# Reloads, sums and result tiles moved in the value projections of a streaming encoder layer

## The chip, the cores and the metric

The kernel runs on one core of one Trainium2 chip. The metric is device time in microseconds, the median of the runs shown. A core has five engines that run their own queues side by side: TensorE (PE, matmuls and transposes, with its weight loads shown apart as PEld), VectorE (DVE), ScalarE (ACT), GpSimd (POOL) and SyncE (SP), which issues most DMAs. An engine works through its queue in order and waits on semaphores for the others.

## The reference

One layer of an encoder over 1024 prompt frames and 64 sample frames (1088 columns in all), model width 1024:

```python
h = rms_norm(x, norm_w) @ w_in                      # 1024 -> 6144 columns
sb_q, sb_k, sb_v, sb_z, cb_q, cb_k, cb_v, cb_z, g_sb, g_cb = split(h)
cb_q, cb_k = rms_norm(cb_q, q_norm_w), rms_norm(cb_k, k_norm_w)   # per head of 64
o_sb = stick_breaking(sb_q, sb_k, sb_v)             # the sample also sees 512 cached keys
o_cb = band_attention(cb_q, cb_k, cb_v, rel_bias)   # chunks of 64, eight chunks to the left
b_sb = (o_sb * silu(sb_z)) @ w_proj_sb
b_cb = (o_cb * silu(cb_z)) @ w_proj_cb
y = x + (sigmoid(g_sb) * b_sb + sigmoid(g_cb) * b_cb) @ w_out
```

It returns y and the new keys and values of both branches, for the prompt and for the sample. All is float32.

## The kernel before, in words

Every float32 product is made of three matmuls on a high and a low part: x = xh + xl and w = wh + wl, and xh*wh + xl*wh + xh*wl is summed in PSUM. A high part is a copy by ACT into a rounded type; the low part is source minus high, by DVE or POOL. The kernel also saves products by Strassen-like sums: a 2x2 block product becomes seven products of sums of blocks, so weights and activations are added before, and results combined after, on DVE.

The order of the work on every engine is the order in which the code is written (a manual schedule). The projections run in three stages.

* **Natural stage** (loop `for i in range(2, nb)`, to about 151 us). For each 256-column block i and each of nine row tiles (index `ti`, with `TO` giving the row tile t, the sample first) PE does 24 matmuls (16 for the sample) into `acc`. `evac_nat` takes squares (ACT, L386), the product with the norm weights and the row sums (DVE, L387 and L389) and the inverse root (POOL, L305 and L306). One tile later `norm_nat` scales the rows (ACT, L398, four pieces), and three tiles later `post_nat` transposes them on PE (L421) into a PSUM tile (`pt`, `pk` or `b2`) and splits the result (ACT L425, DVE L426). Between these, weight quarters for the next stage are loaded (`load_quad`, L523), summed (`sum_w`, L453) and split: `split_quad` makes the high part at once on ACT (L531) and leaves the low part in a list, `lows`, which `put_lows` empties at its next call (L183), on the engine given.
* **Value stage** (`ORDER`, about 151 to 220 us). Twelve steps q, each a product of one weight sum with one activation sum: 48 matmuls at L865, in four parts (q, 0) to (q, 3), and `part(at)` issues the other engines' work ahead of each part. The last four `post_nat` calls fall in the parts of step 0. Activation sums `t2` and `t3` are built late, slice by slice: `fetch(e, ...)` reloads a partial sum from DRAM (`d_t1`, L223), `late_add` adds two activations on DVE (L229 and L230, or L232 and L233), and `late_put` splits it (ACT L238, DVE L183). Results are combined on DVE: L747 into `made`, `u`; L750 into a tile `o` (two buffers in pool `nu`) that SP stores (L719, L721, L723). `sample` makes the sample's rows (L732), and `fold` adds their two halves into an `o` tile (ACT L348, DVE L349).
* **Transposed stage** (from about 220 us). Blocks of 128 columns, seven products each, matmuls at L997. `load_raw` (L466) loads the weights, `presum` (L478) adds them, `prep` splits them (ACT L512, POOL L513). The first five blocks are prepared from parts of the value stage on.

Tiles live in pools that close and give their place to later ones. Where it matters here: at (1, 0) the PSUM pools of `acc`, `pt` and `pk` close and `psB`, with the banks `b1` and `b3` of the value stage, takes their place; at (1, 1) the pool of `hl` closes and the quarters `r00` and `r10` (pool `rw`) are loaded over it, so SP issues their loads only after the stores out of `hl` have landed. At (11, 0) `ndx` with the tiles `dl` closes and `ws` takes its place. `wraw` has two buffers, `d` and `dl` two each.

After the projections come both attentions (about 525 to 820 us) and the output projections; the change does not touch them.

## Time and profile before

| | us |
|---|---|
| median of 3 runs | 961.02 (960.94, 961.02, 962.56) |
| the profiled execution | 961.81 |
| its span, first to last instruction | 960.0 |
| PE busy in the span | 946.9 |
| DVE, ACT, POOL busy | 597.1, 498.7, 383.5 |

How to read a page: the span is cut into busy time per engine; groups of instructions carry their line, engine, operation and tiles (written<-read), and idle time ahead of them stands with what ended it. In a list of waits the row "PE b L865 <- DVE wlo L183: 2.5, 1, 2.5" says that a matmul of line 865 waited 2.5 us in total, once, at most 2.5, for DVE's low part. In a row by time, the start and the duration come first, and "[2.52 <-DVE wlo L183]" is the idle time before it with what ended it. Rows of windows give the stretch, its length, then busy time of PE, PEld, DVE, ACT and POOL with the number of instructions, then the granted clock (1.00 is full), the share of the 16 DMA engines that were busy, and GB/s. "SPq" rows are DMA issues in SP's queue.

### The profile page before, as it was taken

Reading aid. Unit: us, or ns where it says so; the run is one execution under the profiler, and the core shown is the slowest. Engines: PE = TensorE matmul, PEld = TensorE weight load, DVE = VectorE, ACT = ScalarE, POOL = GpSimd, SP = SyncE. Lnnn points to the kernel's source line nnn. Section 1 sums busy time; section 2 is a strip of 40 time slices with the busy share of each in tenths; the row PEclk is TensorE's granted clock in tenths of the full one; section 3 lists DMA queues with packets and bytes.
Section 4 is the critical chain, followed back from the end, with each engine's and each line's share of the span. In section 5 each row is a group of like instructions: output and inputs, shape, how many; then the busy total and the mean of one; then the engine's idle time right before and its main releaser. Section 6 shows DMA issues by size and latency. Waiting matters only on the chain.

```text
span 960.0 us, 20496 instructions
## 1 busy us (share of the span) xinstructions
PE 946.9 (99%) x7547; PEld 900.2 (94%) x7547; DVE 597.1 (62%) x1173; ACT 498.7 (52%) x1151; POOL 383.5 (40%) x386
## 2 busy tenths in 40 slices
PE   9999999899999999999999999999999999999998
PEld 8999999899999999999999987888988988999998
DVE  6656777856454564543332388777777875498735
ACT  7667775323443433333432376667886874565220
POOL 3276665005444566655541200111331112677541
PEclk9999999999999999999999999999999999999999
DMA  7737775574656555556523997679799933852642
GB/s 258 250 129 274 270 250 189 178 230 135 184 165 200 177 164 178 172 158 180 160 91 106 276 251 200 187 184 249 219 302 259 242 102 102 265 172 78 216 136 76
DMA packets 177705, 182.78 MB, mean 190 GB/s; under 512 B 30713, under 2 KB 160125, under 8 KB 177478
## 3 DMA queue, kind: packets, MB, share of 16 engines
q1 hardware_dynamic: 166182, 166.60, 58.1%
q10 hardware_dynamic: 8608, 8.20, 2.6%
q0 software_dynamic: 2816, 6.69, 2.2%
q8 instruction: 60, 0.98, 0.4%
q14 instruction: 39, 0.32, 0.1%
HBM read 117.79 MB, written 63.64 MB: 189 GB/s over the span
## 4 chain that ended last, share of the span: by engine, by line
PE 79%; DMA 6%; DVE 5%; ACT 3%; POOL 2%; issue 1%; SPq 1%; ACTq 1%; DVEq 0%; POOLq 0%
PE b L997 30%; PE o L1519 7%; PE z L1422 7%; PE acc L573 7%; PE pt L1475 7%; PE b L1844 6%; PE acc L1273 5%; PE b L1315 5%; PE acc L1166 2%; PE b L573 1%; DMA d_csbT<-hc 1%; PE b L865 1%; DMA sq<-d_qsbT 1%; POOL rsn L306 1%; DMA ks<-d_ksbT 1%
## 5 line engine op out<-in xcount | busy, mean ns | idle before, releaser
L1475 PE MATMUL pt<-ident,be 128*128 128x128 f32 (+1 forms) x568 | 87.1, 277 | 0.9 <-ACT wT L1484 0.6
L1444 DVE TENSOR_TENSOR_SCAN be<-be,imp 128x128 f32<-128x128 f32 (+7 forms) x64 | 82.7, 1339 | 8.4 <-ACT be L1425 8.3
L1422 PE MATMUL z<-ks,sq 128*128 128x320 f32 (+5 forms) x384 | 87.7, 338 | 0.0
L1484 ACT ACTIVATE wT<-pt 128x512 f32<-128x512 f32 (+3 forms) x123 | 57.1, 497 | 43.8 <-PE pt L1475 43.7
L1475 PEld LDWEIGHTS pt<-ident,be 128*128 128x128 f32 (+1 forms) x568 | 66.2, 140 | 13.8 <-issue 5.3
L997 PE MATMUL b<-xm,wlox 128*128 128x256 f32 (+1 forms) x336 | 76.0, 286 | 0.0
L1005 DVE TENSOR_TENSOR u<-b,s 128x256 f32<-128x256 f32 (+1 forms) x56 | 24.1, 439 | 70.6 <-PE b L997 68.2
L1422 PEld LDWEIGHTS z<-ks,sq 128*128 128x128 f32 x384 | 63.5, 190 | 2.2 <-ACT be L1425 0.9
L1519 PE MATMUL o<-wT,vp 128*64 128x256 f32 (+1 forms) x608 | 64.2, 356 | 0.0
L1519 PEld LDWEIGHTS o<-wT,vp 128*64 128x64 f32 x608 | 40.3, 136 | 22.4 <-issue 5.4
L513 POOL TENSOR_TENSOR wlox<-wraw,wlox 128x512 fp32r<-128x512 f32 x19 | 27.4, 1440 | 76.3 <-ACT wlox L512 76.3
L997 PEld LDWEIGHTS b<-xm,wlox 128*128 128x128 f32 x336 | 56.8, 188 | 0.0
L1447 ACT ACTIVATE be<-be,sm 128x640 f32<-128x640 f32 (+5 forms) x68 | 47.2, 694 | 18.0 <-DVE sm L1446 17.9
L1070 POOL DMA_DIRECT2D d_osb<-zt x20 | 10.9, 543 | 100.9 <-DVE zt L1533 44.4
L513 POOL TENSOR_TENSOR whix<-ws,whix 128x512 fp32r<-128x512 f32 x28 | 37.0, 1320 | 34.6 <-ACT whix L512 30.7
L513 POOL TENSOR_TENSOR wlo<-ws,wlo 128x512 fp32r<-128x512 f32 x28 | 38.9, 1389 | 27.4 <-ACT wlo L512 25.1
L1425 ACT ACTIVATE be<-z 128x384 f32<-128x384 f32 (+6 forms) x104 | 48.1, 517 | 3.4 <-PE z L1422 2.9
L1435 ACT ACTIVATE be<-be,sm 128x640 f32<-128x640 f32 (+5 forms) x68 | 47.3, 696 | 3.8 <-DVE sm L1427 3.3
L1315 PE MATMUL b<-og,whi 128*128 128x384 f32 (+1 forms) x192 | 46.7, 327 | 0.0
L899 ACT ACTIVATE hl<-u 128x256 f32<-128x256 f32 (+1 forms) x40 | 17.0, 432 | 55.8 <-issue 16.7
L997 PE MATMUL b<-t0h,whix 128*128 128x256 f32 (+1 forms) x224 | 44.7, 289 | 0.6 <-POOL whix L513 0.6
L398 ACT ACTIVATE qn<-qn,rsn 128x64 f32<-128x64 f32 (+1 forms) x144 | 38.2, 339 | 13.7 <-POOL rsn L306 13.2
(447 smaller groups left out, 3315.6 us busy)
## 6 DMA issues: line engine op xcount, KB each, us to landing
wraw<-in_w_in_dram SPq DMA_DIRECT2D x34, 512.0 KB, 4.7
wrawx<-in_w_in_dram SPq DMA_DIRECT2D x16, 512.0 KB, 4.4
sq<-d_qsbT SPq DMA_DIRECT2D x32, 192.0 KB, 4.9
sq<-d_qcbT SPq DMA_DIRECT2D x32, 192.0 KB, 5.0
xt<-in_x_prompt_dram SPq DMA_DIRECT2D x8, 512.0 KB, 5.1
d_kcbT<-hl SPq DMA_DIRECT2D x8, 512.0 KB
d_qcbT<-hl SPq DMA_DIRECT2D x8, 512.0 KB
d_ksbT<-hl SPq DMA_DIRECT2D x16, 256.0 KB, 2.7
```

The costliest lines, as they stand in the source:

```text
L513: G.tensor_tensor(out=t[:, 1], in0=src, in1=t[:, 0].bitcast(F32), op=OP.subtract)
L573: TE.matmul(ps, x, w, start=first, stop=last, skip_group_check=i < 2)
L997: TE.matmul(ps[:, :m], w[:, hl_, k], right[s](x)[:, k, a:b], start=s < 3 and k == 0 and e == 0, stop=k == 3 and e == 2, skip_group_check=s ...
L1273: TE.matmul(ps[:, :e - a], w[:, p, cw], g[:, a:e], start=m % 12 == 0, stop=m % 12 == 11)
L1315: TE.matmul(pp[uu][:, :n], w[:, p, uu * 128:uu * 128 + 128], g[:, a:e], start=p == 0 and m == 0, stop=p == NPAIR - 1 and m == 2)
L1422: TE.matmul(z[:, :m], s[:, e, q0:q0 + 128], ks[:, h, o + x:o + y], start=(e, h) == parts[0], stop=(e, h) == parts[-1])
L1425: A.activation(be[:r, x:y], z[:r, :m], AF.Sigmoid, scale=-0.125)
L1444: V.tensor_tensor_scan(be[:r, n - 1::-1], be[:r, n - 1::-1], im[:, ::-1], 0.0, op0=OP.mult, op1=OP.max)
L1475: TE.transpose(pt[:kr, x, :r], be[:r, kb * 128:kb * 128 + kr], ident[:r, :r])
L1484: A.activation(w[:, sl:sl + m, q0:q0 + r], pt[:, :m, :r], AF.Copy)
L1519: TE.matmul(o[hd * 64:hd * 64 + 64, c0:c1], vv[:kr, kb, hd * 64:hd * 64 + 64], wT[b, p, j, hd, s // 4][:kr, s % 4, c0:c1] if j < 4 else wT ...
L1844: TE.matmul(ps[:, t], left[s](xs_, k)[:, ts_], wt_[:, k], start=s < 3 and t == k == e == 0, stop=k == 3 and e == 2, skip_group_check=s > 2 ...
```

## The change

In the natural stage's last block: the sums of weight quarters are made one or two tiles earlier, the low part of the first is made by DVE and no longer by POOL, the split of quarter 3 stands ahead of the last tile's `evac_nat` with its low part on DVE, and row tile 6 transposes into `pk`, not `pt`. In the value stage: `fetch(2)` stands ahead of the quarters and goes to the `d` tiles of pool `tq`, `fetch(3)` goes there too, later, `fetch(4)` and `fetch(5)` go to `dl`, the last two to `d`; the reload of quarter (0, 1, 1) moves from (7, 0) to (2, 1); `load_raw(2)` moves from (9, 2) to (11, 1). The two results of step 9 go to `dl` tiles, the first result of step 11 and the fold of the second sample to `made` tiles allocated anew at (10, 1). The low part of block 1 is made by DVE. The core of the diff:

```diff
-            if raw1[:2] == (nb - 1, 7):
+            if raw1[:2] == (nb - 1, 7) and t != 6:
                 pt = psT.tile([128, 4, 128], F32, name="pt")
...
+                if (i, ti) == (nb - 1, 8):
+                    split_quad(3, quad[0, 0, 1])
+                    put_lows()
                 got = evac_nat(i, t, ps)
...
-                if (i, ti) == (nb - 1, 2):
+                if (i, ti) == (nb - 1, 1):
                     for n in (1, 2):
                         made[n] = pn.tile([128, 4, 256], F32, name=f"made{n}", bufs=1)
                     sum_w(made[1], quad[0, 0, 1], quad[0, 1, 1], OP.add)
                     load_quad(0, 1, 0, wpool, "wraw", 2)
+                if (i, ti) == (nb - 1, 2):
+                    sum_w(made[2], made[1], quad[0, 0, 0], OP.subtract)
+                    split_quad(0, made[2])
                 if (i, ti) == (nb - 1, 4):
-                    sum_w(made[2], made[1], quad[0, 0, 0], OP.subtract)
-                    split_quad(0, made[2], G)
-                if (i, ti) == (nb - 1, 5):
                     sum_w(quad[0, 0, 0], quad[0, 0, 0], quad[0, 0, 1], OP.subtract)
                     split_quad(1, made[1])
+                if (i, ti) == (nb - 1, 6):
+                    sum_w(quad[0, 1, 0], quad[0, 1, 0], made[2], OP.subtract)
                 if (i, ti) == (nb - 1, 7):
-                    sum_w(quad[0, 1, 0], quad[0, 1, 0], made[2], OP.subtract)
                     load_quad(1, 1, 1, pn, "made1", 1)
...
-                if (i, ti) == (nb - 1, 8):
-                    split_quad(3, quad[0, 0, 1], G)
-                    put_lows()
...
-                put_s(j, 1, fold(nu.tile([128, 512], F32, name="o")[0:64], ps))
+                lo = made[1][0:64, 0:2].rearrange("p t n -> p (t n)") if j else nu.tile([128, 512], F32, name="o")[0:64]
+                put_s(j, 1, fold(lo, ps))
...
-            v = nu.tile([128, 512], F32, name="o")
+            if (j, s) == (1, 4):
+                v = nd.tile([128, HF], F32, name="dl")[:, :512]
+            elif (j, s, c) == (0, 5, 0):
+                v = made[2][:, 0:2].rearrange("p t n -> p (t n)")
+            else:
+                v = nu.tile([128, 512], F32, name="o")[:]
...
             elif at == (1, 1):
+                fetch(2, tq, "d")
                 p1hx.close()
...
                 load_quad(1, 0, 0, rw, "r00", 1)
-                fetch(2, nd, "dl")
                 load_quad(1, 1, 0, rw, "r10", 1)
-                fetch(3, nd, "dl")
...
                 split_quad(4, made[1])
+                fetch(3, tq, "d")
                 late_add(2)
...
                 for e in (4, 5):
-                    fetch(e, tq, "d")
+                    fetch(e, nd, "dl")
+                load_quad(0, 1, 1, wpool, "wraw", 2)
...
                 for e in (6, 7):
-                    fetch(e, nd, "dl")
+                    fetch(e, tq, "d")
...
                 split_quad(10, quad[1, 1, 1])
-                load_quad(0, 1, 1, wpool, "wraw", 2)
...
                 load_raw(1)
-                load_raw(2)
+            elif at == (10, 1):
+                for n in (1, 2):
+                    made[n] = pn.tile([128, 4, 256], F32, name=f"made{n}", bufs=1)
...
                 presum(1)
-                prep(1)
+                prep(1, V)
+            elif at == (11, 1):
+                load_raw(2)
```

What it moves, at three places. First DVE, from the split of row tile 3 (`hl<-pk`, the end of the natural stage) to that of row tile 7; the new low part is that of quarter 3, and L387 with L389 are the norm steps of tile 7:

```order
 L426 TENSOR_TENSOR hl<-pk,hl 128x2x128
+L183 TENSOR_TENSOR wlo<-wraw,whi 128x1024
 L387 TENSOR_TENSOR qn<-acc,wqk 128x256
 L389 TENSOR_REDUCE msn<-sqn 128x4
 L426 TENSOR_TENSOR hl<-pt,hl 128x2x128 x2
-L747 TENSOR_TENSOR made_296<-b_2571,made_296 128x512
-L426 TENSOR_TENSOR hl<-pt,hl 128x2x128
+L749 TENSOR_TENSOR made_296<-b_2571,made_296 128x512
+L426 TENSOR_TENSOR hl<-pk,hl 128x2x128
 L183 TENSOR_TENSOR wlox<-wraw,whix 128x1024
 L426 TENSOR_TENSOR hl<-pt,hl 128x2x128
```

The low part of quarter 3 has come ahead of tile 7's norm, and tile 6's transposes are read from `pk`.

Second SP's queue at parts (1, 1) to (2, 1), before. The first two rows are the last stores out of `hl`; `r` are the quarters, `d` and `dl` the reloads, `u` the partial result:

```order
L53 DMA d_qcbT_68<-hl 256x1x512
L53 DMA d_qcbT_69<-hl 256x1x512
L523 DMA r_2702<-in_w_in_dram 128x4x256
L223 DMA dl<-d_t_129 128x544
L523 DMA r_2706<-in_w_in_dram 128x4x256
L223 DMA dl<-d_t_130 128x544
L787 DMA u_2710<-d_s_126 128x1024
L223 DMA d<-d_t_127 128x544
```

And the same place in the change:

```order
L53 DMA d_qcbT_68<-hl 256x1x512
L53 DMA d_qcbT_69<-hl 256x1x512
L223 DMA d<-d_t_129 128x544
L523 DMA r_2704<-in_w_in_dram 128x4x256
L523 DMA r_2706<-in_w_in_dram 128x4x256
L793 DMA u_2708<-d_s_126 128x1024
L223 DMA d<-d_t_130 128x544
L223 DMA dl<-d_t_127 128x544
L223 DMA dl<-d_t_128 128x544
L523 DMA wraw<-in_w_in_dram 128x4x256
```

The first reload has passed both quarters, the second has fallen behind them and behind `u`, and the late quarter `wraw` has come up.

Third DVE at the results of steps 7, 9 and 10 (`b` are PSUM banks), in the change; before, the rows with `dl` and `made_3196` wrote `o`:

```order
L757 TENSOR_TENSOR o<-b_3049,made_2513 128x512
L757 TENSOR_TENSOR o<-b_3080,made_2513 128x512
L757 TENSOR_TENSOR dl<-b_3120,u_2709 128x512
L183 TENSOR_TENSOR wlox<-wraw,whix 128x1024
L757 TENSOR_TENSOR dl<-b_3155,u_2709 128x512
L757 TENSOR_TENSOR o<-b_3120,u_2708 128x512
L757 TENSOR_TENSOR o<-b_3155,u_2708 128x512
L349 TENSOR_TENSOR made_3196<-acc,made_3196 64x256
L478 TENSOR_TENSOR ws<-wraw 128x512
```

The order is the old one; the tiles written are others.

## The prediction

> **What bounds the kernel now.** I read the page's busy line first, then the waits of TensorE, then busy time by windows, then the order of time around each wait.

> ```profile
> PE 946.9 (99%) x7547; PEld 900.2 (94%) x7547; DVE 597.1 (62%) x1173; ACT 498.7 (52%) x1151; POOL 383.5 (40%) x386
> ...
> PE b L865 <- DVE wlo L183: 2.5, 1, 2.5
> PE pt L421 <- DVE hl L426: 1.9, 1, 1.9
> PE b L997 <- POOL whix L513: 0.6, 1, 0.6
> PE b L865 <- issue: 0.6, 1, 0.6
> PE b L865 <- DVE o L750: 0.3, 1, 0.3
> ...
> 168.00:180.00 12.00, 9.48 (x69) 9.29 (x69) 9.01 (x12) 3.43 (x4) 0.00 (x0) 0.86 0.64 232
> 180.00:200.00 20.00, 20.00 (x172) 20.00 (x172) 19.76 (x26) 7.38 (x9) 0.00 (x0) 1.00 0.37 122
> ```

> PE (TensorE) is busy for 946.9 of 960.0 us: it is the bound, and a change that leaves its matmuls as they are can win only its idle time and its slow time. The change edits only the stretch from about 135 to 230 us, and there the five waits above are all of PE's idle time. The first window row has a granted clock of 0.86: slow time too. The second says what to fear: in 180 to 200 VectorE (DVE) is busy 19.76 of 20 us, so once PE stops waiting DVE has little to give.

> **The wait at 155 (sums sooner, own bank for one transpose).** Rows by time:

> ```profile
> 152.00 1.07 ACT L398 ACTIVATE qn<-qn,rsn 128x64 f32<-128x64 f32 x4 [2.60 <-POOL rsn L306]
> 155.11 1.04 ACT L531 ACTIVATE whi<-wraw 128x1024 fp32r<-128x1024 f32 x1
> 156.58 1.06 ACT L398 ACTIVATE qn<-qn,rsn 128x64 f32<-128x64 f32 x4
> 157.80 1.05 ACT L531 ACTIVATE whix<-wraw 128x1024 fp32r<-128x1024 f32 x1
> 158.89 1.23 DVE L183 TENSOR_TENSOR wlox<-wraw,whix 128x1024 fp32r<-128x1024 f32 x1 [0.52 <-ACT whix L531]
> 160.03 0.42 DVE L426 TENSOR_TENSOR hl<-pt,hl 128x256 fp32r<-128x256 f32 x1
> 147.34 2.40 POOL L183 TENSOR_TENSOR wlo<-made,whi 128x1024 fp32r<-128x1024 f32 x1
> 154.89 1.01 POOL L306 TENSOR_TENSOR rsn<-rsn,half 128x4 f32<-128x4 f32 x1
> 156.92 0.44 PE L421 MATMUL pt<-ident,qn 128*128 128x128 f32 x2 [1.90 <-DVE hl L426]
> 161.13 0.28 PE L865 MATMUL b<-whix,t0h 128*128 128x256 f32 x1
> ```

> PE waits at 156.92 because tile 6's transposes need a `pt` bank that tile 4 still holds. The change gives tile 6 the `pk` bank, which tile 3 leaves earlier: that wait goes. What is late next is tile 7, whose transposes come twelve matmuls on (12 x 0.115 us), at about 156.5. Its normalised rows come from ACT (L398, 156.58 to 157.64 before). Two things now pull at that row. POOL's 2.40 us lo part (147.34) goes to DVE, at 1.22 us; the rsqrts of tiles 5 and 6 no longer queue behind it, so ACT's 2.60 us of idle at 152.00 shrinks. Against that, the 1.04 us split (155.11) moves ahead of tile 7's Square on ACT, and its lo part (1.22) ahead of tile 7's product and reduce on DVE. Adding the rows: PE ends tile 7's matmuls at the old 151.4; split on ACT to 153.2; lo on DVE to 154.4; two 0.41 us norm steps to 155.1; rsqrt on POOL (before, to 155.90) to about 156.5. So L398 starts near 156.5, as before. PE then waits some 1.1 us here, not 1.9. Behind this row ACT still runs the copy of tile 6, the split at 157.80, and DVE the 1.23 at 158.89 and the copy at 160.03, ending at 160.45. Step 1's first matmul (161.13) needs that, since its bank is taken from the transposes' pool. So it starts at about 160.6: gain **0.5 us** (bounds: 0, if tile 7 slips by the moved 1.22; 1.9, if it comes in time).

> **The wait at 172 (reloads ahead of quarters).**

> ```profile
> 160.47 1.18 SPq L53 DMA_DIRECT2D d_qcbT<-hl  x2
> 166.50 0.39 SPq L523 DMA_DIRECT2D r<-in_w_in_dram  x1
> 166.94 0.50 SPq L223 DMA_DIRECT2D dl<-d_t  x1
> 162.66 0.73 DVE L183 TENSOR_TENSOR t2l<-d,t2h 128x544 fp32r<-128x544 f32 x1 [0.23 <-issue]
> 171.64 0.72 DVE L229 TENSOR_TENSOR dl<-dl,xa 128x544 f32<-128x544 f32 x1 [2.92 <-DMA dl<-d_t]
> 173.65 1.22 DVE L183 TENSOR_TENSOR wlo<-r,whi 128x1024 fp32r<-128x1024 f32 x1
> 172.12 0.28 PE L865 MATMUL b<-whi,t0l 128*128 128x256 f32 x1
> 174.91 0.38 PE L865 MATMUL b<-wlo,t0h 128*128 128x256 f32 x1 [2.52 <-DVE wlo L183]
> 165.00:167.00 2.00, 2.00 (x20) 2.00 (x19) 1.24 (x3) 0.66 (x1) 0.00 (x0) 1.00 0.06 25
> 168.00:171.00 3.00, 3.00 (x29) 3.00 (x29) 0.72 (x1) 1.06 (x1) 0.00 (x0) 1.00 0.97 337
> d<-d_t SPq DMA_DIRECT2D x4, 272.0 KB, 6.7
> 176.00:177.00 1.00, 1.00 (x6) 1.00 (x6) 1.00 (x2) 0.27 (x1) 0.00 (x0) 0.50 0.02 7
> ```

> DVE stands 2.92 us at L229 for a reload that SP issued only at 166.94: SP had waited from 161.65 to 166.50 until the stores of 160.47 had landed, because the quarter ahead of the reload is written where their source lay. Behind L229, in DVE's order, is the 1.22 us lo part that PE wants. In the change the reload has the `d` buffer of an earlier pool and stands ahead of the quarter. It needs only that DVE is done with that buffer, at 163.4 (162.66 and 0.73); landing 4.70 us after issue (166.94 to 171.64) it is there at 168.1, when DVE comes to it. So lo ends at 173.65 + 1.22 - 2.92, less the 0.5 by which step 1's results, that DVE takes in between, come earlier: 171.4. PE, also 0.5 earlier, wants it at 171.7 (172.12 + 0.11 - 0.5). The wait goes, with 0.3 us to spare: 174.91 - 172.12 less a normal 0.11, **2.7 us**. Bounds: 1.0, if the reload takes 6.7 us like the `d` reloads (then DVE is 2.0 us late and PE waits 1.7); 2.7.

> What is late next is the second such reload. It now stands behind both quarters and the 512 KB `u` load, not behind one quarter and a reload. That is 3 x 512 and 272 KB, 1.85 MB, at the 0.34 MB per us of 168 to 171: 5.5 us. In the trace the first reload, with 0.8 MB ahead of and in it (2.3 us), landed 5.1 us after the quarter's issue at 166.50, so some 2.8 us are issue and landing: 8.3 us in all, from an issue that moves to about 165.3 with the stores ahead of it: 173.6. DVE comes to it after the lo of 171.4, a 0.73 and a 1.22 us step: 173.3. From 173.6 it needs 0.72, 0.73, 0.69 and 1.22 us to the end of the next lo part (lox), 176.9. PE wants that 50 matmuls of 0.115 on from 171.5: 177.2. Priced at nothing, with 0.3 us of cover; without that cover it costs what it is late.

> **The half clock.** In 176 to 177 the clock is 0.50 and PE starts 6 matmuls instead of about 9. The slow stretch follows that wait:

> ```profile
> 175.82 0.37 PE L865 MATMUL b<-whi,t0h 128*128 128x256 f32 x1
> 179.19 0.32 PE L865 MATMUL b<-whi,t0l 128*128 128x256 f32 x1
> ```

> That is 3.37 us and 16 steps, 0.21 us each where 0.115 is usual: 16 x 0.095, **1.5 us**. No such stretch follows the 1.9 us wait at 155. I take it as caused by the longer wait, and gone with it.

> [...]

> **The three waits from 205 on (tiles of their own, raw loads, V for one lo part).**

> ```profile
> 205.13 0.28 PE L865 MATMUL b<-wlox,t2h 128*128 128x256 f32 x1
> 206.05 0.36 PE L865 MATMUL b<-whi,t3h 128*128 128x256 f32 x1 [0.64 <-issue]
> 208.83 0.28 PE L865 MATMUL b<-wlo,t3h 128*128 128x256 f32 x1
> 209.44 0.38 PE L865 MATMUL b<-whi,t3h 128*128 128x256 f32 x1 [0.33 <-DVE o L750]
> 225.98 0.28 PE L997 MATMUL b<-t0l,whix 128*128 128x256 f32 x1
> 226.91 0.51 PE L997 MATMUL b<-t0h,whix 128*128 128x256 f32 x2 [0.65 <-POOL whix L513]
> 205.25 0.69 DVE L750 TENSOR_TENSOR o<-b,u 128x512 f32<-128x512 f32 x1 [2.95 <-DMA out_dram<-o]
> 224.28 0.38 ACT L348 ACTIVATE o<-acc 64x256 f32<-64x256 f32 x1 [3.40 <-DMA out_dram<-o]
> ```

> DVE's L750 stands 2.95 us for one of the two `o` tiles to be stored, and PE starts 0.11 after it ends. With `dl` tiles for these two results that wait cannot occur; the matmul before is the limit. Excess over a normal 0.115: 0.81 and 0.49, with 0.17 for the slow restarts: 1.5. At 226.91 POOL's whix waited for ACT, which stood 3.40 us for an `o` tile before it; with the sample's fold and one result in `made` tiles ACT's step is due some 10 us earlier. The excess is 0.81 and 0.12: 0.9. Together **2.4 us**. The moved lo part adds 0.7 us to DVE at about 210, in a stretch where it stood waiting for `o` tiles. The `ws` tiles lie where the `dl` tiles were, so they now wait for two stores; the stores land near 208, and the part is wanted at 216.

> **Sum.** 0.5 + 2.7 + 1.5 + 2.4 = 7.1 us; I take off 0.1 for two margins of 0.3 us that may not hold: 7.0. No matmul, no byte and no split is added, so nothing else is charged. The profiled execution took 961.81 us, 1.81 around its span of 960.0; 961.81 - 7.0 = 954.8. The median shown is 961.02, 0.79 lower: **954.0 us**.

> **Rivals.**
> 1. DVE becomes the bound: a reload or lo part comes 1 to 2 us later than in my sums. For it: 19.76 of 20 us busy, and margins of 0.3. Against: DVE's queue also moves some 3.5 us ahead (171.64 to 168.1). PE then waits 0.6 to 1.6 at 172 or 177; 955.0 to 956.0, and with a half clock 957.5. Chance 0.22.
> 2. [...] Chance 0.07.
> 3. The change does not do what it says: the reload, though issued early, lands only after the stores of 160.47 and the quarters, so 172 and its clock stay. Only 0.5 and 2.4 remain: 958.1. Against it: the DMA share is 0.06 in 165 to 167, so the stores are through by then. Chance 0.06.
> 4. Slower: the second reload, now fourth in SP's line, holds DVE at L229 and with it lox, wlo and the next lox, one after another. It decides from the point where the wait at 177 costs more than the 7.0 gained: with 1.5 for the clock, 5.5 us plus 0.3 of cover, a landing near 179, 12 us after issue. The `d` reloads took 6.7. 963. Chance 0.03.

> My forecast (953 to 955) has 0.62. What a run can tell from no change is about 0.2%, 1.9 us: faster means under 959.1. The forecast, rivals 1, 2 and most of 3 lie there: 0.93 with rounding; same 0.04, slower 0.03. The range holds 8 in 10 with the forecast, rival 2 and most of rival 1: below to 952.5, where tile 7 comes in time (1.4 more); above to 957.5, rival 1 with its half clock.

> **What would show it.** Right: TensorE's waits between 150 and 230 show one of about 1 us at L421, for ACT's qn and not for a bank, and none over 0.5 elsewhere; the granted clock in 168 to 180 is 1.00; DVE's L229 has no wait for a DMA of 2 us; DVE's late results wait for no store. Wrong: a wait of over 1 us on a wlo or wlox of L183 (rival 1, or 3 if DVE's wait for the reload is still there); a clock of 0.5 anywhere in the stretch (rival 2); L229 waiting for the second reload past 175 (rival 4); new waits outside 135 to 230, on which I count none.

## The result, and the profile after

The changed kernel takes 955.71 us in the median of four executions (954.02 to 956.25), the kernel before beside it 961.59 (960.94 to 962.56): a ratio of 0.9935, with an interval of 0.9918 to 0.9952. A second set of runs gave 956.15 (six executions, 953.97 to 957.49) against 961.34, a ratio of 0.9943 (0.9931 to 0.9956). The kernel is faster by 5 to 6 us. Forecast were 954.0, 7.0 less than the median shown, in a range of 952.5 to 957.5.

The profiled execution took 954.02 us. Its busy line, TensorE's waits (in total, times, longest) and two rows of windows, which answer those shown of before:

```profile
PE 944.7 (99%) x7547; PEld 899.1 (94%) x7547; DVE 596.2 (63%) x1176; ACT 498.4 (52%) x1151; POOL 379.6 (40%) x383
...
PE pt L421 <- ACT qn L398: 0.7, 1, 0.7
...
PE b L876 <- DVE wlox L183: 0.2, 1, 0.2
PE b L876 <- DVE hl L426: 0.2, 1, 0.2
...
168.00:180.00 12.00, 11.82 (x101) 11.61 (x100) 10.25 (x14) 3.45 (x4) 0.00 (x0) 1.00 0.81 286
180.00:200.00 20.00, 20.00 (x173) 20.00 (x172) 19.76 (x27) 8.34 (x10) 0.00 (x0) 1.00 0.33 108
```

The five waits of 150 to 230 have become three small ones (L876 is the L865 of before). PE's granted clock in 168 to 180 is 1.00 where it was 0.86. VectorE is as full as before in 180 to 200: 19.76 of 20 us.

VectorE and the DMA queue by time, in the same execution:

```profile
163.24 0.77 SPq L223 DMA_DIRECT2D d<-d_t  x1
166.60 0.94 SPq L523 DMA_DIRECT2D r<-in_w_in_dram  x2
167.59 0.50 SPq L793 DMA_DIRECT2D u<-d_s  x1
168.19 0.38 SPq L223 DMA_DIRECT2D d<-d_t  x1
...
168.04 0.72 DVE L229 TENSOR_TENSOR d<-d,xa 128x544 f32<-128x544 f32 x1
...
170.04 1.22 DVE L183 TENSOR_TENSOR wlo<-r,whi 128x1024 fp32r<-128x1024 f32 x1
...
174.70 0.73 DVE L229 TENSOR_TENSOR d<-d,xa 128x544 f32<-128x544 f32 x1 [1.68 <-DMA d<-d_t]
...
176.70 1.21 DVE L183 TENSOR_TENSOR wlox<-r,whix 128x1024 fp32r<-128x1024 f32 x1
...
200.30 0.68 DVE L757 TENSOR_TENSOR dl<-b,u 128x512 f32<-128x512 f32 x1
...
202.03 0.68 DVE L757 TENSOR_TENSOR dl<-b,u 128x512 f32<-128x512 f32 x1
...
207.56 0.69 DVE L757 TENSOR_TENSOR o<-b,u 128x512 f32<-128x512 f32 x1 [2.44 <-DMA out_dram<-o]
```

The first reload is issued 3.4 us ahead of the quarters, and L229 at 168.04 waits for nothing, where it stood 2.92 us at 171.64. The second reload comes late: L229 at 174.70 stands 1.68 us for it. The results of step 9 (L757, tiles `dl`) wait for no store. The second result of step 10, still in an `o` tile, stands 2.44 us for one, and no wait of PE follows: of the late results, the prediction's sign "wait for no store" holds for step 9 alone.

So far the steps of the prediction seem to hold one by one, except for 1.1 to 1.8 us. The experiments show that one of its terms cost the kernel before nothing that can be measured, that another was there in one profile of three, and that two others cannot be added up.

### The profile page after: what moved, and what is told of

Read it like the earlier page. It is cut to its first block, busy times and chain, and to the rows that moved or that the text cites. A ratio compares the mean times of both kernels' runs of the same rounds, so it can differ in the third digit from the quotient of the medians.

```text
span 952.2 us, 20492 instructions
## 1 busy us (share of the span) xinstructions
PE 944.7 (99%) x7547; PEld 899.1 (94%) x7547; DVE 596.2 (63%) x1176; ACT 498.4 (52%) x1151; POOL 379.6 (40%) x383
## 3 DMA queue, kind: packets, MB, share of 16 engines
q1 hardware_dynamic: 166182, 166.60, 58.7%
## 4 chain that ended last, share of the span: by engine, by line
PE 94%; DMA 2%; ACT 1%; DVE 1%; issue 0%; POOL 0%; SPq 0%; DVEq 0%; ACTq 0%; POOLq 0%
PE b L1008 31%; PE acc L573 12%; PE b L1855 8%; PE o L1530 7%; PE z L1433 7%; PE pt L1486 7%; PE acc L1284 5%; PE b L1326 5%; PE acc L1177 4%; PE b L876 4%; PE b L573 1%; PE pt L334 1%; DMA d<-d_t 1%; DMA d_qcbT<-hl 1%; PE acc L1898 1%; PE b L421 1%
## 5 line engine op out<-in xcount | busy, mean ns | idle before, releaser
L513 POOL TENSOR_TENSOR wlox<-wraw,wlox 128x512 fp32r<-128x512 f32 x19 | 28.0, 1473 | 78.6 <-ACT wlox L512 78.6
L513 POOL TENSOR_TENSOR whix<-ws,whix 128x512 fp32r<-128x512 f32 x28 | 36.6, 1307 | 40.7 <-ACT whix L512 40.4
L398 ACT ACTIVATE qn<-qn,rsn 128x64 f32<-128x64 f32 (+1 forms) x144 | 38.2, 339 | 13.8 <-POOL rsn L306 13.5
L1008 PE MATMUL b<-t3h,whi 128*128 128x256 f32 (+1 forms) x224 | 44.6, 289 | 0.0
```

Source lines behind the costliest of these rows:

```text
L513: eng.tensor_tensor(out=t[:, 1], in0=src, in1=t[:, 0].bitcast(F32), op=OP.subtract)
L1008: TE.matmul(ps[:, :m], w[:, hl_, k], right[s](x)[:, k, a:b], start=s < 3 and k == 0 and e == 0, stop=k == 3 and e == 2, skip_group_check=s ...
```

## The experiments

Diffs are against the changed kernel, unless another is named. Beside medians I use the length of one stretch of a trace: from the first matmul of the value stage to the first transpose of the new keys (line 923 before, 934 after the change, some 15 us into the transposed stage, behind the edits' last place). It leaves out what the other 870 us do, which is about 1 us in either direction from one execution to the next. The first four experiments were timed on one chip, where the kernel before takes 961.0 and the changed kernel was not run; so their distance from the changed kernel is given by the medians, and also by the gains over the kernel before in each set of runs (5.9 and 5.2 for the changed kernel).

### The reloads

**All reloads back in their old order and tiles** (the later ones too, which the lines shown leave out), the other parts of the change kept:

```diff
             elif at == (1, 1):
-                fetch(2, tq, "d")
                 p1hx.close()
...
                 load_quad(1, 0, 0, rw, "r00", 1)
+                fetch(2, nd, "dl")
                 load_quad(1, 1, 0, rw, "r10", 1)
+                fetch(3, nd, "dl")
...
-                fetch(3, tq, "d")
                 late_add(2)
```

> The changed kernel with the reloads back in their old places (fetch 2 and 3 between and behind the quarters, into dl; 4 and 5 into d, 6 and 7 into dl); all else as changed. My theory: the wait for DVE's lo part at step 4 is back at 2.5 to 2.9 us and the half clock with it (1.5), less the 0.45 that the second reload costs the changed kernel at step 5: about 3.8 us slower than the changed kernel, 959.5, clock 0.998. Rival: the half clock has nothing to do with this wait: the clock stays at 1.00 and it is 2.2 us slower, 957.9. Rival (DVE is the bound): the wait is back but what PE loses here it would have lost at steps 5 and 6 anyway: under 1.5 us slower.

Measured: 959.29 (957.09 to 960.31, 11 executions), a ratio to before of 0.9978 (0.9969 to 0.9987); 3.1 to 3.6 above the changed kernel by the medians, 3.5 to 4.2 by the gains. Of its profile, the wait, its rows by time, and a window:

```profile
PE b L876 <- DVE wlo L183: 2.4, 1, 2.4
...
172.41 0.72 DVE L229 TENSOR_TENSOR dl<-dl,xa 128x544 f32<-128x544 f32 x1 [3.10 <-DMA dl<-d_t]
...
174.41 1.21 DVE L183 TENSOR_TENSOR wlo<-r,whi 128x1024 fp32r<-128x1024 f32 x1
...
168.00:180.00 12.00, 9.64 (x69) 9.44 (x68) 8.84 (x12) 3.43 (x4) 0.00 (x0) 0.86 0.77 268
```

The wait and the half clock are back, behind VectorE's 3.10 us for the reload. The order and the tiles of the reloads alone decide this wait: shown. The time is as expected, and so is the clock of this profile.

**The kernel before with the new order and tiles of the reloads**, and nothing else (the same lines, the other way round):

> The kernel before with nothing but the reloads moved (fetch 2 ahead of the quarters, fetch 3 behind u, both into d; 4 and 5 into dl, 6 and 7 into d). My theory: the 2.5 us wait at step 4 and the half clock behind it go, some 0.2 to 0.4 come back at step 5: 4.0 us faster than before, 957.5; the waits of 1.9 at L421 and of 0.6, 0.3 and 0.6 behind 205 us stay as they were. Rival (the reload lands only after the stores): no gain, 961.5. Rival (the clock does not follow the wait): 2.5 us faster, 959.0.

Measured: 959.57 (958.19 to 961.4, 11 executions), ratio 0.9981 (0.9972 to 0.999). It gains 1.4, not the 4.0 expected. The wait at 172 is gone and the clock there is 1.00, but another has grown. PE's wait, the row of it, VectorE ahead of it, and a window:

```profile
PE b L865 <- issue: 2.5, 1, 2.5
...
199.61 1.28 DVE L750 TENSOR_TENSOR o<-b,made 128x512 f32<-128x512 f32 x2
203.79 0.69 DVE L750 TENSOR_TENSOR o<-b,u 128x512 f32<-128x512 f32 x1 [2.90 <-DMA out_dram<-o]
...
204.58 0.55 PE L865 MATMUL b<-whi,t3h 128*128 128x256 f32 x1 [2.51 <-issue]
...
200.00:220.00 20.00, 17.49 (x140) 17.32 (x139) 7.87 (x12) 2.70 (x4) 2.56 (x2) 0.91 0.77 241
```

PE comes to step 10 at 202.1 instead of 205.4, and stands there for the `o` tiles until 204.6 instead of 206.05; a stretch at half clock begins here. VectorE's two results are made at 199.61 instead of 200.94, only 1.3 us earlier, since VectorE is full from 180 on (19.76 of 20 us, as before), and the next result still waits 2.90 us for the store. What the reloads win at 172 is paid back at 205.

### The result tiles

**All late results and the fold in `o` tiles again:**

```diff
-            if (j, s) == (1, 4):
-                v = nd.tile([128, HF], F32, name="dl")[:, :512]
-            elif (j, s, c) == (0, 5, 0):
-                v = made[2][:, 0:2].rearrange("p t n -> p (t n)")
-            else:
-                v = nu.tile([128, 512], F32, name="o")[:]
+            v = nu.tile([128, 512], F32, name="o")[:]
```

> The changed kernel with all late results and both folds back in the two o tiles; the moved raw loads, the early quarter and the lo part on DVE stay. My theory: DVE stands for the stores of o again, PE waits 0.8 and 0.5 us at the two halves of step 10, and ACT's fold holds the split for the third product of the transposed stage, 0 to 0.9: 1.3 to 2.2 us slower than the changed kernel, 957.0 to 957.9. Rival: the moved raw loads took the pressure from the stores, and the tiles do nothing: 955.7, the same as the changed kernel.

Measured: 958.65 (956.91 to 960.03, 11 executions), ratio 0.9975 (0.9966 to 0.9984): 2.5 to 2.9 above the changed kernel by the medians, 2.8 to 3.5 by the gains, where 1.3 to 2.2 were expected. PE's wait and the window:

```profile
PE b L868 <- issue: 2.8, 1, 2.8
...
200.00:220.00 20.00, 17.18 (x134) 17.01 (x133) 7.93 (x12) 1.64 (x3) 1.27 (x1) 0.91 0.74 233
```

With everything ahead of it earlier, the old wait of 0.64 is 2.8 us, and a half clock follows it here. By the medians on this chip (before: 961.0) the reloads alone gain 1.4 and the rest without them 1.7, while both together gain 5 to 6: each has its worth only with the other.

### The natural stage

**The sums, the splits and the bank of row tile 6 as before:**

```diff
-            if raw1[:2] == (nb - 1, 7) and t != 6:
+            if raw1[:2] == (nb - 1, 7):
...
-                if (i, ti) == (nb - 1, 8):
-                    split_quad(3, quad[0, 0, 1])
-                    put_lows()
                 got = evac_nat(i, t, ps)
...
-                    split_quad(0, made[2])
+                    split_quad(0, made[2], G)
```

> The changed kernel with its part in the natural stage undone: sums and splits at their old places, low parts 0 and 3 on POOL, tile 6 back in pt. My theory: the 1.9 us wait at L421 for a bank takes the place of the 0.7 for tile 7's rows, and step 1 starts 0.5 later: 0.5 us slower, 956.2. Rival: what is lost is the difference of the waits, 1.2 us or more: 956.9. Rival: no difference, since DVE's copies and the lox of step 2 decide when step 1 starts: 955.7.

Measured: 955.78 (954.19 to 957.47, 5 executions), ratio 0.9944 (0.993 to 0.9957), as the changed kernel. The wait at 155 is back, and PE waits more at 178 too:

```profile
PE pt L421 <- DVE hl L426: 1.7, 1, 1.7
...
PE b L875 <- DVE wlox L183: 0.9, 1, 0.9
```

That this part gains nothing is not shown, only that it is not more than about 1 us: in this profile some 190 of PE's matmuls (161 to 178 us, 196 to 201.5) ran at the shorter of two measured paces (below), 0.1133 us each where the changed kernel's profile has 0.1178, and that hides about 0.9 us.

### The raw loads and the low part of block 1

```diff
                 load_raw(1)
+                load_raw(2)
...
-                prep(1, V)
-            elif at == (11, 1):
-                load_raw(2)
+                prep(1)
```

> The changed kernel with two edits taken back: the second raw load stands at part (9, 2) again, and the low part of block 1 is GpSimd's again. My sum had 0.9 us for the wait at the start of the transposed stage and put it down to the fold's tile, not to these two edits: then this run takes what the changed kernel takes, 955.7 within 0.7, and TensorE waits for no whix or wlo at the start of that stage. Rival: the 0.9 belongs to them; then the wait is back at 215 to 222, 0.6 us or more, and the time is about 956.6.

Measured: 954.6 (953.34 to 955.74, 5 executions) against 960.28 for the kernel before beside it, ratio 0.9937 (0.9923 to 0.9952). There is no wait for a `whix` at the start of the transposed stage. These two edits change nothing that can be measured. Two further profiles of the kernel before (below) do not have that wait either, so that the 0.65 us of the profile I predicted from was that execution's. ACT stands ahead of the fold (L348) in all three (3.40 us, then 3.37 and 3.17), but only in the first does PE wait in the end.

### Is the half clock due to the length of the wait?

**The changed kernel, with one result of VectorE in step 2 made five, or seven, times** (the sum is the same):

```diff
-                    V.tensor_tensor(out=two(u[j, "23"[e - 1]]), in0=banks[j, e, c], in1=two(u[j, "2"]), op=OP.add)
+                    for _ in range(5 if (j, s, e, c) == (0, 2, 2, 1) else 1):
+                        V.tensor_tensor(out=two(u[j, "23"[e - 1]]), in0=banks[j, e, c], in1=two(u[j, "2"]), op=OP.add)
```

> The changed kernel with one of VectorE's results of step 2 (0.6 us) made five times in place of once, so that the low part for step 4 comes some 2.4 us later and TensorE waits about 2.0 us for it at 174. Theory A (the half clock follows any single wait of TensorE from some length between 1.9 and 2.4 us on): no half clock, the granted clock stays 1.00 in 168 to 180, and the time is 2.0 over the changed kernel's. Theory B (it needs a fixed window of about 3.4 us that is mostly idle, and where the wait lies in it decides): a half clock may come here though the wait is shorter than that of 2.4, with 1.5 us more, 3.5 in all.

> The same with seven in place of one, so that the low part comes some 3.6 us later and TensorE waits about 3.2 us. Theory A: a half clock of about 3.4 us follows at once, and the time is 3.2 + 1.5 = 4.7 us over the changed kernel's, with a granted clock of about 0.86 in 168 to 180. A third view, that only a wait longer than 3.4 us brings a half clock, has none here: 3.2 over.

> The run with the low part made 2.4 us late once more, now timed several times for the granted clock of each execution: one stretch of 3.4 us at half clock in a span of 955 us lowers its mean from 1.000 or 0.999 to 0.998. Theory A (the half clock follows a wait of more than some 2.1 to 2.4 us): the wait of 2.1 is too short every time, all clocks are 0.999 or 1.000. Theory B (windows of about 3.4 us that run free, halved behind one in which TensorE idled for more than some part): whether the 2.1 us fall into one window is chance, so that some of the executions show 0.998, and these take about 1.5 us more than the others. Time in the median: 957.6 by A, 957.6 to 958.4 by B.

Measured with five: 957.62 in one execution, then 957.58 (957.03 to 959.07, six executions), ratio 0.9971 (0.9959 to 0.9982). Both profiles have the same wait. Of the first, the matmul behind the wait and the window:

```profile
175.00 0.38 PE L877 MATMUL b<-wlo,t0h 128*128 128x256 f32 x1 [2.08 <-DVE wlo L183]
...
168.00:180.00 12.00, 9.92 (x84) 9.72 (x84) 11.79 (x16) 3.44 (x4) 0.00 (x0) 1.00 0.72 256
```

and of the second, the wait in the list of TensorE's and the window:

```profile
PE b L877 <- DVE wlo L183: 2.1, 1, 2.1
...
168.00:180.00 12.00, 9.93 (x72) 9.72 (x71) 11.79 (x16) 3.45 (x4) 0.00 (x0) 0.86 0.72 258
```

PE is busy as long in both, but starts 84 matmuls in one and 72 in the other. Of the seven executions five have a granted clock of 0.998 or 0.997, two have 1.000. With the half clock the stretch to the transposes is 81.18 us, without 79.16. By their whole time the five are on average 0.4 us longer than the two (957.78 against 957.41), not the 1.5 that theory B gave; seven executions that differ by 2 us are too few to tell these apart. So of two profiles with the same wait of 2.1 us one has a half clock behind it and the other none, and by the granted clocks five of the seven executions had one: theory A, a length from which it always comes and below which it never does, has fallen for this length.

With seven: 959.65 us, and a wait of 3.5:

```profile
175.69 0.58 PE L877 MATMUL b<-wlo,t0h 128*128 128x256 f32 x1 [3.52 <-DVE wlo L183]
...
168.00:180.00 12.00, 8.48 (x56) 8.27 (x55) 11.73 (x17) 3.43 (x4) 0.00 (x0) 0.77 0.64 228
```

The granted clock is 0.50 from 174.39 to 181.22, twice 3.41 us; it began inside the wait (172.17 to 175.69). The time is 3.5 to 3.9 us over the changed kernel, between the 3.2 and the 4.7 expected, in a single execution. The third view, that only a wait longer than 3.4 us brings a half clock, has fallen by the wait of 2.1, as by the 2.5 in the kernel before.

Where the clock changes says more. In each of the fourteen traces kept, the record of the granted clock begins, with 1.00, at a point between 5.2 and 7.3 us (5.18 before, 6.72 after), another one in each execution, and every later change of it lies a whole number of times 3.413 us behind that point: 50 and 51 times in the kernel before, 58 and 59 times with the tiles undone. To the waits it has no fixed distance. In the kernel before the stretch began 0.9 us after the wait's end, with the tiles undone also 0.9 after, with the reloads undone 0.4 after, and with the reloads alone at 204.09, 0.5 ahead of it. A delay counted from the wait would be one number.

This grid separates the two profiles with five. Here are the two stretches of 3.41 us that the wait touches in the first, then the one with the wait and the next in the second:

```profile
170.53:173.95 3.42, 2.39 (x21) 2.19 (x19) 3.28 (x6) 0.48 (x1) 0.00 (x0) 1.00 0.99 367
173.95:177.36 3.41, 2.36 (x20) 2.36 (x21) 3.40 (x4) 0.55 (x1) 0.00 (x0) 1.00 0.87 316
...
172.58:175.99 3.41, 1.34 (x12) 1.29 (x12) 3.38 (x5) 0.00 (x0) 0.00 (x0) 1.00 0.99 362
175.99:179.41 3.42, 3.42 (x19) 3.42 (x18) 3.39 (x5) 1.72 (x2) 0.00 (x0) 0.50 0.07 24
```

In the first a boundary cuts the wait: PE is idle for 1.0 us in each of two windows, and the clock stays full. In the second the whole wait lies in one window, 2.07 us of it idle, and the next window is at half clock. Over all fourteen traces every window at full clock with 2.02 to 2.53 us of idle time (seven of them) was followed by one at half clock, and none with up to 1.55 us was (1.55 in 155.37 to 158.78 of the kernel before, with 1.00 behind it); in between none was seen. In the run with seven a window that was itself at half clock, with 1.3 us of idle time, was followed by a second one. In these traces, then, it is the idle time inside one window of this grid that goes with the half clock, and not the length of the wait.

### What did the half clock cost in the kernel before?

In the three sets of runs that list the clock of every execution, the kernel before ran 48 times: 29 times at 0.998 or less, 13 times at 1.000 and six at 0.999. One stretch of 3.41 us at half clock lowers the mean over 958 us to 0.998 (half of 3.41 is 0.18% of 958), so that by this estimate the last two groups have none. Within each set the first group is 0.18 us longer, 1.35 shorter and 1.03 longer than those at 1.000; together that is 0.02 us with a standard error of 0.3 (0.06 with the six counted in). A term of 1.5 us is excluded. With the reloads undone and the result tiles in place it is different: six executions at 0.998 or less have a mean of 959.66, the other five of 958.37.

To see where the 1.5 us goes, **the kernel before was profiled twice more**, unchanged:

> The kernel before once more, for its trace. Of its timed executions some have a granted clock of 0.998 or less and some of 1.000, and both take the same time. If the stretch at half clock is a matter of chance and its 1.5 us are given back, a trace without it must show TensorE arriving about 1.5 us earlier at step 10 and standing there 2 us or more for the o tiles, not 0.64. If it is not given back, that wait stays near 0.6 and the trace is 1.5 us shorter there. About one execution in four has no such stretch, so that this look and the next may both show the trace that is known already.

> The kernel before a third time, with the same expectation as the look above: a wait of 2 us or more at step 10 where the half clock is absent, of about 0.6 where it is there.

Measured: 960.21 and 960.46 us. The first has the stretch at half clock. Its waits of TensorE:

```profile
PE b L865 <- DVE wlo L183: 2.6, 1, 2.6
PE pt L421 <- DVE hl L426: 1.6, 1, 1.6
...
PE b L865 <- issue: 0.5, 1, 0.5
PE b L865 <- DVE o L750: 0.5, 1, 0.5
```

The second has none, with its window and the row of VectorE that ends the wait at step 10:

```profile
PE b L865 <- issue: 2.0, 1, 2.0
PE b L865 <- DVE wlo L183: 1.9, 1, 1.9
PE pt L421 <- DVE hl L426: 1.7, 1, 1.7
...
PE b L865 <- DVE o L750: 0.7, 1, 0.7
...
168.00:180.00 12.00, 10.05 (x86) 9.85 (x85) 9.25 (x12) 3.44 (x4) 0.00 (x0) 1.00 0.66 233
...
205.28 0.69 DVE L750 TENSOR_TENSOR o<-b,u 128x512 f32<-128x512 f32 x1 [2.92 <-DMA out_dram<-o]
```

Without the half clock the wait at step 10 is 2.0 us instead of 0.5, and the stretch to the transposes is 82.88 us without and 82.77 with it. What PE lost to its clock it had back at step 10, where it would have stood for VectorE's `o` tile anyway. The times of the 48 executions show that the term was nobody's loss; the two traces, one of each kind, show where it went.

### The changed kernel again, and a version with two steps moved

```diff
+                got = evac_nat(i, t, ps)
                 if (i, ti) == (nb - 1, 8):
                     split_quad(3, quad[0, 0, 1])
                     put_lows()
-                got = evac_nat(i, t, ps)
...
                 load_quad(1, 1, 0, rw, "r10", 1)
+                fetch(3, tq, "d")
...
                 split_quad(4, made[1])
-                fetch(3, tq, "d")
                 late_add(2)
```

> The changed kernel itself once more, beside the two below and the kernel before on the same chip. If its 955.7 is what the kernel takes, it comes out between 954.8 and 956.5, 4.5 to 6.5 us under the kernel before; if the median of four runs was lucky or unlucky with the two paces of matmuls (0.1133 and 0.1175 us each), it comes out 1 us or more away.

> The changed kernel with two steps moved again: the split of quarter 3 with its low part stands behind the last tile's norm steps, not ahead of them, and the second reload is issued right behind the two quarters, ahead of u. My theory says that TensorE's 0.7 us wait for ACT's qn at the transposes of tile 7 is the 1.04 us split and the 1.22 us low part ahead of that tile's norm; with the norm first the qn comes about 1 us sooner and the wait is under 0.2. The reload then lands about 172.9 instead of 174.7, VectorE's wait of 1.68 us at L229 falls under 0.5, and TensorE's wait of 0.2 for wlox goes. Together 0.9 to 1.1 us less: 954.7 where the changed kernel takes 955.7. Rival: step 1's start is held by the evacuations behind the transposes and not by the transposes (the rows of 160.32 show a wait of 0.17 for hl), and the reload's lateness cost nothing in the end: then the waits go and the time stays within 0.3 of the changed kernel's.

Measured: the changed kernel 956.15, as given above, and this version 953.8 (952.59 to 954.69, six executions), a ratio to before of 0.992 (0.9908 to 0.9931). It beats both kernels: 7.5 us under the one before, 2.35 under the changed one, where 0.9 to 1.1 were expected. TensorE's waits in the changed kernel's profile of that set:

```profile
PE pt L421 <- ACT qn L398: 1.1, 1, 1.1
PE b L876 <- DVE wlox L183: 0.5, 1, 0.5
```

and, for the version, all that is left of them, its window, and the row that stood 1.68 us:

```profile
PE b L876 <- DVE hl L426: 0.2, 1, 0.2
...
168.00:180.00 12.00, 12.00 (x104) 12.00 (x104) 11.90 (x16) 4.68 (x6) 0.00 (x0) 1.00 0.93 323
...
173.16 0.72 DVE L229 TENSOR_TENSOR d<-d,xa 128x544 f32<-128x544 f32 x1
```

Both waits are gone, and L229 waits for no transfer. The stretch to the transposes is 76.22 us, against 78.51 and 77.85 in the two profiles of the changed kernel. The waits were larger than the first profile had them (1.6, not 0.9), which explains the larger part of the 2.35; the rest, some 0.7 us, has no cause that was tested. Some 0.4 of it may be the shorter pace of TensorE's matmuls (below; 0.0045 us for each of some 100 of them), which this profile has from 195.5 us on and the two of the changed kernel only from 208 and 209. The two moves were made together, so that the share of each is not known.

## Why the prediction was right or wrong

**The direction and the range** held: faster, with 955.7 inside 952.5 to 957.5. The forecast itself, 954.0, was 1.7 us too low (2.1 by the second set). That it came so near is in part luck: two terms that were not there, 1.5 and 0.9, were partly made up by the result tiles, which were worth more than their term. The time is also the one that rival 1 named, 955.0 to 956.0, but the waits of 0.6 to 1.6 us that it gave for it were not there. Term by term:

* **2.7 for the wait at 172: right as to the mechanism**, and shown by taking the reloads back. The reload goes ahead of the quarters, lands before VectorE comes to it, and the wait is gone.
* **1.5 for the half clock: wrong.** The step that failed is "I take it as caused by the longer wait, and gone with it", used as a term of the sum. It did follow the wait and did go with it, but it came in 29 of 48 executions of the kernel before, and cost them nothing that can be measured (0.02 us, standard error 0.3), since the wait at step 10 shrank by as much. A price of 1.5 was right only for a kernel in which nothing behind it waits. I had read the cause off a single trace. The seven executions with one and the same edit, 5 with the stretch and 2 without, and the grid of 3.413 us on which the clock changes in every trace, show that the wait alone did not bring it.
* **1.5 of the 2.4 for the late results: right as to the mechanism, mis-sized**: 2.5 to 3.5 when taken back, with a half clock that then comes behind the wait. In the sum, what PE wins at 172 was counted as if it were kept up to 230, while the wait at 205 ends with VectorE and a store, not with PE. Excess of a wait now in the trace is not its price when PE comes earlier: 0.5 became 2.0 without the half clock, and 2.5 with the reloads moved. As all parts were made at once, this error and that of the half clock partly cancel.
* **0.9 of the 2.4 for the wait at 226.9: wrong.** The step that failed is "POOL's whix waited for ACT, which stood 3.40 us", read as a wait of PE in every execution. ACT stands about as long in all three profiles of the kernel before, and PE waits in one of them.
* **0.5 for the wait at 155: not settled.** The wait that was forecast (about 1.1 us at L421, for ACT's qn) is there, 0.7 and 1.1 in two profiles; what it gains in time is too small for these runs. The order that the sum found fault with, the split and its low part ahead of tile 7's norm, was the right suspect: that order turned round is part of the fastest version.
* **Nothing for the second reload: wrong by 0.4 to 0.7.** It landed at 174.7 (and 175.9 in the second profile), not at 173.6. The step that failed is "an issue that moves to about 165.3 with the stores ahead of it": the quarters were issued at 166.60, as late as before, since the stores out of `hl` moved by only 0.2 us (160.29 for 160.47). The 8.3 us from there to the landing were right: they took 8.1. VectorE stood 1.68 and 1.96 us, and PE 0.2 and 0.5 at `wlox`; in the first profile the matmul behind that wait took 0.22 us to the next, not 0.12 (177.97 and 178.19). This is rival 1 on a small scale; no clock of 0.5 came in the stretch (rival 2), nor did rivals 3 and 4.

Without the 1.5 and the 0.9, and with 0.5 for the second reload, the sum is 4.2 by its own rows; with the price of the result tiles that was measured (2.7 in place of 1.5) 5.4; the two sets of runs show 5.9 and 5.2. That it fits proves little: 2.7 is the price of the tiles once the reloads have moved, and by the experiments these terms do not add up.

## What to carry to other kernels

Waits on one chain of engines are not terms to be added: before summing, follow the engine that ends each wait (here VectorE, full for 20 us, and a store) and ask how much earlier it can be, since what the stalled engine wins upstream it may stand for downstream. The same holds for losses: a slow clock ahead of a wait that another engine ends was free here (0.02 us, standard error 0.3). And a wait that is to carry a term should be seen in more than one execution.

## What the runs showed of the hardware

At a granted clock of 1.00 TensorE's 256-column matmuls of the value stage were seen at two pitches. The first and the last of four matmuls in a row of step 0 before, and of six in a row of step 2 after, by time:

```profile
159.77 0.28 PE L865 MATMUL b<-whi,t1h 128*128 128x256 f32 x1
...
160.11 0.28 PE L865 MATMUL b<-whi,t1h 128*128 128x256 f32 x1
```

```profile
166.09 0.28 PE L876 MATMUL b<-whix,xm 128*128 128x256 f32 x1
...
166.67 0.28 PE L876 MATMUL b<-wlox,xm 128*128 128x256 f32 x1
```

That is 0.34 us for three matmuls and 0.58 for five, 0.113 and 0.116 us each; over 3 us at a time the means are 0.1133 and 0.1178 us, 4% apart. In six profiles of the value stage (three of the kernel before, the changed kernel, and the runs with the natural stage and the raw loads undone) a pace held for 2 to 46 us (from 161 to 207 in the changed kernel). Each change but one (at 201.5, with the natural stage undone) came at a wait, at the sample's matmuls or in the stretch at half clock, in either direction, and not the same in two executions of one kernel: the kernel before had the shorter from 160 us on in two profiles, in the third only from 198 on. Steps 1 and 2 took 10.88 us in the profile before and 11.42 in that after: the pace of their 96 matmuls is 0.43 of these 0.54 us; the rest is the first matmul of step 1, which in the profile after, behind a wait of 0.17 us, took 0.23 us to the next and not 0.12 (160.32 and 160.55). (Steps 3 and 8 have no matmuls at this line; the other ten of the twelve have 48 each.) It may be one source of the 2 to 4 us between executions of one kernel, which was not tested; what sets the pace stays open too.
